# A hybrid attention decoder layer on one core: operand sums made early and kept in DRAM, and four small edits

## The chip, the core and the metric

The kernel runs on one core of one Trainium2 chip. The metric is the device time of one execution in microseconds. Each time is the median of several executions; before the change it is 897.02 us (three executions, 896.83 to 897.15). Engine names are those of the profile: PE is TensorE (matmuls), PEld its weight loads, DVE is VectorE, ACT is ScalarE, POOL is GpSimd, SP is SyncE, which here only issues DMAs.

## What is computed

One decoder layer on 512 tokens of width 1024, in float32. The parts that matter here:

```python
h = layer_norm(x, ln_in_g, ln_in_b)
q_g, k_g, v_g, r_g, a_lr, q_lat, kv_lat, gate_logits = split(h @ w_in)
y_gla = gated_linear_attention(q_g, k_g, v_g, a_lr, r_g) @ w_o_gla       # 4 heads
q = rms_norm(q_lat) @ w_q_b;  kv = rms_norm(kv_lat) @ w_kv_b             # latent attention, 8 heads
s = (q_nope @ k_nope.T + rope(q_rope) @ rope(k_rope).T) * scale          # causal, blocks of 128 queries
y_mla = merge_heads(softmax(s) @ v) @ w_o_mla
g_gla, g_mla = split(sigmoid(gate_logits + b_gate))                      # 1024 channels each
h = layer_norm(alpha * h + (g_gla * y_gla + g_mla * y_mla) @ w_out, ln1_g, ln1_b)
out = layer_norm(alpha * h + square(relu(h @ w_ff1)) @ w_ff2, ln2_g, ln2_b)
```

GLA is the gated linear attention, MLA the latent attention.

## The kernel before, in words

**Precision.** Nearly every product is made of three matmuls. A float32 operand x is split in two parts, hi (rounded, made by ACT) and lo = x - hi (made by DVE); the product is hi*hi + hi*lo + lo*hi, accumulated in PSUM. `split` (L109, its two operations at L111 and L112) does it for activations, `pump` (L177) for weights: L189 is the hi part of a weight block, L190 the lo part.

**The weight stream.** All weight blocks (512 KB each, mostly) stand in one list, `stream`. `fetch` issues their loads on SP's queue (L174) into three buffers (`wraw`), `pump(i)` brings the list to block i and somewhat beyond. `gemm_fm` (matmuls at L245 to L247, 512 tokens moving) and `gemm_tm` (L278 to L280, weights moving) call it before each use, and once more in the middle of the evacuation of their results.

**Order.** The program is written as one main thread of GEMMs and several generators (`spawn`, `tick`, `finish`); each `tick` lets the first two to four generators go one step, so that their small instructions fall between the matmuls. On top of that, a scheduler reorders each engine's instructions by a timeline that it simulates; `tc.issue_after(x)` holds the instructions inside it behind x. On the chip each engine then runs its list strictly in that order.

**Stages**, by their time in the profile: input LayerNorm and latent projections (to 47 us), the q and k products of GLA (47 to 94), v and r (94 to 213), the four GLA heads worked through beside these and the next stage (`gla_levels`: a scan in eight doubling steps, on POOL at L677 and L678, ACT at L682, DVE at L684 and L694, PE at L738), the GLA gates as two GEMMs of 8 blocks (213 to 273), the MLA gates (to 316), rotary queries and the output projection of GLA (from 316 and 320), the MLA heads (354 to 509), output projection and LN1 (to 572), the MLP (to 844), and the last projection (to 887) with LN2.

**Operand sums of the MLA gates.** The MLA gates are computed by a scheme of seven half-size products instead of eight (`unit` L1007, matmuls at L1028 to L1030). It needs sums and differences of quarters of the operand h (`op_sums`, L975): DVE adds the hi and lo part of h (L980), forms four combinations per pair of channel blocks (L984 to L987), and each is split again (L111, L112). `h_sums` runs it beside the two GEMMs of the GLA gates; `u_load("g1", "t1")` ahead of these GEMMs loads two weight blocks on SP and has POOL issue two further loads that are added onto them (L1005).

**Rotary queries.** `mla_qr` (L813) computes the rotary part of four heads' queries; on evacuation DVE does three `rope` operations (L498 to L500) and POOL one for each of the four token blocks. The next GEMM is the first half of the GLA output projection.

**Scores.** `mla_head` (L859) works over four blocks of 128 queries. Block i reads n = 128(i+1) keys; the first block's five matmuls (L871 to L875) are done 256 keys wide. The causal mask is a sixth, bf16 matmul (L876).

**LN1.** `ln_transpose` (L414) transposes the normalised rows on PE (L421); ACT writes the hi part (L424), DVE the float32 copy (L428) and the lo part (L429), eight channel blocks for each half of the tokens.

**The end.** The last 128 tokens of the last projection are done in three column groups of 512, 256 and 256 (L1413 to L1415). Each is added to the residual (L1417), its statistics are taken (L1419), and `ln2` (L1208) applies LN2 in two halves of 512 columns (L1220, L1221) and stores them (L1222).

Of the kernel before, what the change touches and what calls it, by code (L numbers as in the profile page):

```python
# [52 lines left out]
def tile_hybrid_block(ctx: ExitStack, tc: tile.TileContext, I, out, dbg=None):  # L53
# [360 lines left out]
    def ln_transpose(rows, g, b, outs, hf, alt=False, n="h0"):  # L414
        tk = slice(hf * 256, (hf + 1) * 256)
        for k in range(NK):
            if len(outs) <= k:
                outs.append(A([P, 2, T], F32R, n) if n == "h0" else (B([P, T], F32R, n), B([P, T], F32R, n)))
            p = MM() if alt and k in (4, 5) else PX()
            for i in range(2):  # L420
                nc.tensor.transpose(p[:, i * P:(i + 1) * P], rows[2 * hf + i][:, k * P:(k + 1) * P], ident)  # L421
            tmp = B([P, 256], F32, "lnt")
            hi, lo = part(outs[k], 0, tk), part(outs[k], 1, tk)
            ha = act(hi, p[:, :256], AF.Identity, scale=g[:, k:k + 1], bias=b[:, k:k + 1])  # L424
# [388 lines left out]
    def mla_qr(g):  # L813
        qst = []

        def ev_qr(a, j, ps):
            src = ps[:, :4 * ROPE].rearrange("p (h c) -> p h c", c=ROPE)
            csb = cs2[:, a, None, :].to_broadcast([P, 4, ROPE])
            snb = sn2[:, a, None, :].to_broadcast([P, 4, ROPE])
            t1 = B([P, 4, ROPE], F32, "rt1")  # L820
            t2 = B([P, 4, ROPE], F32, "rt2")
            rope(src, csb, snb, t1, t1, t2)
            q2 = B([P, 4, 2, ROPE], F32R, "q2")
            split(t1, q2[:, :, 0, :], q2[:, :, 1, :], scale=scale)
# [12 lines left out]
        return spawn(tr())  # L837
# [21 lines left out]
    def mla_head(h, hl, qn, kn, vt):  # L859
        for _ in range((0 if h == MH - 1 else STAG) * hl):  # L860
            yield
        KK, qs = KKs[0], QS[h]
        Ps = []
        P02 = B([P, T], F32, "P02")
        for i in range(NT):
            n = P * (i + 1)
            nn = max(n, 2 * P)
            c = slice(i * P, (i + 1) * P)
            p = PX()
            o = p[:, :nn]  # L870
            mm(o, qn[:, 0, c], kn[:, 0, :nn], start=True, stop=False)  # L871
            mm(o, qn[:, 0, c], kn[:, 1, :nn], start=False, stop=False)
            mm(o, qn[:, 1, c], kn[:, 0, :nn], start=False, stop=False)
            mm(o, qs[:, c], KK[:, 0, :nn], start=False, stop=False)
            mm(o, qs[:, c], KK[:, 1, :nn], start=False, stop=False)  # L875
# [24 lines left out]
        while vt[NT - 1] is None:  # L900
            yield
        o = PX()
        for j in range(NT):
            c = slice(hl * P, (hl + 1) * P)
            vh, vl = vt[j][:, 0, c], vt[j][:, 1, c]
            if j == 0:
                ph, pl, od = PT0[:, 0, :], PT0[:, 1, :], o
            elif j == 1:
                ph, pl, od = PT1[:, 0, :384], PT1[:, 1, :384], o[:, 128:]
            elif j == 2:  # L910
                ph, pl, od = PT2[:, 0, :], PT2[:, 1, :], o[:, 256:]
            else:
                ph, pl, od = PT1[:, 0, 384:], PT1[:, 1, 384:], o[:, 384:]
            mm(od, vh, ph, start=j == 0, stop=False)
            mm(od, vh, pl, start=False, stop=False)
            mm(od, vl, ph, start=False, stop=j == NT - 1)
        yield
        om = A([P, 2, T], F32R, "omT")
        st["om"] = split(o, om[:, 0, :], om[:, 1, :])
        omT[h] = om  # L920


    def ln_in1():
# [9 lines left out]
        yield  # L933
        yield from ln_transpose(xt, g_in, b_in, hT, 1, alt=False)

    t_ln1 = spawn(ln_in1())
    t_prep = None
    for hf in range(2):
# [133 lines left out]

    hops = []

    def h_sums():
        yield from op_sums(hT,
                           lambda: [[B([P, 2, 256], F32R, "sh") for _ in range(2)] for _ in range(2)], hops)

    t_h = spawn(h_sums())
    u_load("g1", "t1")  # L1080
    for mb in range(2):
        gemm_fm(PL["g", 0, mb], hT, T, lambda a, ps: gate(0, 4 * mb + a, ps, slice(0, T)))
    finish(*t_gla)

    def after(op):
# [119 lines left out]
            yield  # L1205


    def ln2(tt, bst=None):  # L1208
# [130 lines left out]
    for ci in range(FC):  # L1339
# [34 lines left out]
        else:  # L1374
# [29 lines left out]
            gemm_tm(PL["f2last"], hid, T, ev_res, tts=(2,))  # L1404
            spawn(ln2(2))
            tt, r, bst = 3, res[3], S([P, 4, 6], F32, "bst4")
            for c0, n in ((0, T), (T, 256), (T + 256, 256)):
                acc = MM()[:, :n]
                ws = slice(c0 % T, c0 % T + n)
                for k in range(nb):  # L1410
                    hi, lo = weights(PL["f2last"][c0 // T], k)
                    xh, xl = hid[k][:, 0, tt * P:], hid[k][:, 1, tt * P:]
                    mm(acc, xh, hi[:, ws], start=k == 0, stop=False)  # L1413
                    mm(acc, xh, lo[:, ws], start=False, stop=False)
                    mm(acc, xl, hi[:, ws], start=False, stop=k == nb - 1)  # L1415
                    tick(None)
                vtt(r[:, c0:c0 + n], acc, r[:, c0:c0 + n], op=ALU.add)  # L1417
                for j in range(c0 // 256, (c0 + n) // 256):
                    nc.vector.bn_stats(bst[:, j, :], r[:, j * 256:(j + 1) * 256])  # L1419
            finish(spawn(ln2(3, bst)))  # L1420


# [46 lines left out]
```

## Time and profile before

| | |
|---|---|
| median of the executions | 897.02 us |
| the profiled execution | 896.5 us |
| its span, first to last instruction | 894.7 us |
| PE busy | 877.5 us (98%) |
| DVE busy | 614.5 us (69%) |
| ACT busy | 445.1 us (50%) |
| POOL busy | 170.4 us (19%) |
| HBM | 107 GB/s over the span |

The profile is one execution. Its span leaves out 1.8 us around the first and the last instruction. PE's ends of matmuls are modelled, so that back-to-back matmuls overlap in the records; how long one really takes is the distance between the starts of two neighbours. An idle time of PE of half a microsecond or so shows as a wait, a smaller one only in the distance between starts.

### The profile page before, as it was taken

Reading aid. Unit: us, or ns where it says so; the run is one execution under the profiler, and the core shown is the slowest. Engines: PE = TensorE matmul, PEld = TensorE weight load, DVE = VectorE, ACT = ScalarE, POOL = GpSimd, SP = SyncE. Lnnn points to the kernel's source line nnn. Section 1 sums busy time; section 2 is a strip of 40 time slices with the busy share of each in tenths; the row PEclk is TensorE's granted clock in tenths of the full one; section 3 lists DMA queues with packets and bytes.
Section 4 is the critical chain, followed back from the end, with each engine's and each line's share of the span. In section 5 each row is a group of like instructions: output and inputs, shape, how many; then the busy total and the mean of one; then the engine's idle time right before and its main releaser. Section 6 shows DMA issues by size and latency. Waiting matters only on the chain.

```text
span 894.7 us, 12542 instructions
## 1 busy us (share of the span) xinstructions
PE 877.5 (98%) x4796; PEld 760.5 (85%) x4796; DVE 614.5 (69%) x1003; ACT 445.1 (50%) x757; POOL 170.4 (19%) x190
## 2 busy tenths in 40 slices
PE   6999999999999999999999999999999999999996
PEld 5988888888889988888888888988888888889986
DVE  7835855577775745747756797997556646787866
ACT  6455543443546543535645423366457546656810
POOL 1003442444531010100000002103400520141000
PEclk9999999999999999999999999999999999999999
DMA  7314413216325723112207618004950991399312
GB/s 246 122 47 163 131 60 95 71 48 152 84 71 175 197 87 102 49 55 58 95 25 260 210 48 305 3 0 118 314 135 3 271 257 35 76 231 236 117 62 82
DMA packets 73037, 109.41 MB, mean 122 GB/s; under 512 B 7904, under 2 KB 42080, under 8 KB 72976
## 3 DMA queue, kind: packets, MB, share of 16 engines
q1 hardware_dynamic: 57520, 76.62, 27.1%
q0 software_dynamic: 13536, 28.32, 13.8%
q10 hardware_dynamic: 1920, 3.66, 1.2%
q8 instruction: 38, 0.62, 0.3%
q14 instruction: 23, 0.19, 0.1%
HBM read 91.28 MB, written 4.72 MB: 107 GB/s over the span
## 4 chain that ended last, share of the span: by engine, by line
PE 97%; DVE 1%; DMA 1%; ACT 0%; issue 0%; DVEq 0%
PE mm L245 12%; PE mm L247 12%; PE mm L246 12%; PE mm L278 7%; PE mm L279 7%; PE mm L280 7%; PE mm L1030 3%; PE mm L1029 3%; PE mm L1028 3%; PE px L1288 2%; PE px L1287 2%; PE px L1286 2%; PE px L738 2%; PE mm L1288 2%; PE mm L1287 2%; PE mm L1286 2%
## 5 line engine op out<-in xcount | busy, mean ns | idle before, releaser
L190 DVE TENSOR_TENSOR wlo<-wraw,whi 128x1024 fp32r<-128x1024 f32 (+1 forms) x98 | 110.4, 1127 | 110.0 <-ACT whi L189 102.4
L189 ACT ACTIVATE whi<-wraw 128x1024 fp32r<-128x1024 f32 (+1 forms) x98 | 93.9, 959 | 97.9 <-PE mm L246 48.9
L245 PE MATMUL mm<-h,whi 128*128 128x512 f32 x288 | 112.7, 392 | 0.0
L246 PE MATMUL mm<-h,whi 128*128 128x512 f32 x288 | 112.4, 390 | 0.0
L247 PE MATMUL mm<-h,wlo 128*128 128x512 f32 x288 | 107.1, 390 | 0.0
L1305 POOL DMA_DIRECT2D res<-ev x42 | 37.4, 1003 | 177.9 <-ACT ev L1303 143.6
L245 PEld LDWEIGHTS mm<-h,whi 128*128 128x128 f32 x288 | 54.0, 188 | 11.0
L246 PEld LDWEIGHTS mm<-h,whi 128*128 128x128 f32 x288 | 54.1, 188 | 10.8
L247 PEld LDWEIGHTS mm<-h,wlo 128*128 128x128 f32 x288 | 53.9, 188 | 11.0
L279 PE MATMUL mm<-wlo,h 128*128 128x512 f32 x128 | 50.3, 393 | 0.0
L280 PE MATMUL mm<-whi,h 128*128 128x512 f32 x128 | 50.1, 392 | 0.0
L190 DVE TENSOR_TENSOR wlo<-wq,whi 128x1024 fp32r<-128x1024 f32 x30 | 36.7, 1225 | 19.4 <-ACT whi L189 19.4
L278 PE MATMUL mm<-whi,h 128*128 128x512 f32 x128 | 49.7, 403 | 0.0
L677 POOL TENSOR_TENSOR rp<-rp 128x256 f32<-128x256 f32 x32 | 31.6, 988 | 61.1 <-ACT E L682 44.8
L189 ACT ACTIVATE whi<-wq 128x1024 fp32r<-128x1024 f32 x30 | 31.7, 1058 | 19.7 <-PE mm L1029 11.4
L189 ACT ACTIVATE xh<-wraw 128x1024 fp32r<-128x1024 f32 (+1 forms) x28 | 27.4, 984 | 27.8 <-PE mm L280 16.3
L684 DVE TENSOR_TENSOR M<-E,qk 128x512 f32<-128x512 f32 x32 | 27.8, 868 | 14.1 <-ACT E L682 14.1
L406 POOL TENSOR_TENSOR mv<-mv,mhalf 128x1 f32<-128x1 f32 x4 | 4.6, 1155 | 172.3 <-DVE mv L405 172.3
L190 DVE TENSOR_TENSOR xl<-wraw,xh 128x1024 fp32r<-128x1024 f32 (+1 forms) x28 | 31.3, 1130 | 8.5 <-ACT xh L189 8.4
L1028 PE MATMUL mm<-sh,whi 128*128 128x256 f32 x128 | 36.2, 283 | 0.0
L1029 PE MATMUL mm<-sh,whi 128*128 128x256 f32 x128 | 36.2, 283 | 0.0
L1030 PE MATMUL mm<-sh,wlo 128*128 128x256 f32 x128 | 36.2, 283 | 0.0
(419 smaller groups left out, 2576.9 us busy)
## 6 DMA issues: line engine op xcount, KB each, us to landing
wraw<-in_w_in_dram SPq DMA_DIRECT2D x38, 512.0 KB, 3.5
wraw<-in_w_ff_dram SPq DMA_DIRECT2D x36, 512.0 KB, 5.1
wq<-in_w_ff_dram POOLq DMA_DIRECT2D x26, 512.0 KB, 9.7
res<-ev POOLq DMA_DIRECT2D x42, 256.0 KB, 9.2
wraw<-in_w_o_gla_dram SPq DMA_DIRECT2D x8, 512.0 KB, 3.7
wraw<-in_w_o_mla_dram SPq DMA_DIRECT2D x8, 512.0 KB, 3.5
wraw<-in_w_out_dram SPq DMA_DIRECT2D x8, 512.0 KB, 3.8
wq<-in_w_in_dram SPq DMA_DIRECT2D x6, 512.0 KB, 6.1
```

What stands on the lines that cost most here:

```text
L189: st["ins"] = act(hi[:, :nk, :n], raw[:, :nk, :n], AF.Copy)
L190: st["lo"] = vtt(lo[:, :nk, :n], raw[:, :nk, :n], f(hi[:, :nk, :n]), op=ALU.subtract)
L245: mm(o, hi[:, c], xh, start=first, stop=False)
L246: mm(o, hi[:, c], xl, start=False, stop=False)
L247: mm(o, lo[:, c], xh, start=False, stop=last)
L278: mm(o, xh, hi[:, :n], start=opens, stop=False, skip_group_check=share)
L279: mm(o, xh, lo[:, :n], start=False, stop=False, skip_group_check=share)
L280: mm(o, xl, hi[:, :n], start=False, stop=last, skip_group_check=share)
L1028: mm(oa, hi[:, k, c], xh, start=opens and k == 0 and a == 0, stop=False, skip_group_check=True)
L1029: mm(oa, hi[:, k, c], xl, start=False, stop=False, skip_group_check=True)
L1030: mm(oa, lo[:, k, c], xh, start=False, stop=k == 3, skip_group_check=True)
L1305: nc.gpsimd.dma_start(res[tt + t][:, j * T:(j + 1) * T], e, accum_op=ALU.add)
```

## The change

Six edits:

1. The operand sums are made by a new generator `h_early`, started before the k product, with buffers of another pool. Each split part (128x512, 256 KB) is stored to DRAM on SP's queue, 16 stores. `h_load` takes the place of `h_sums`: 16 loads on SP's queue into the buffers that `unit` reads.
2. `u_load("g1", "t1")` moves from ahead of the two GEMMs of the GLA gates to between them.
3. `mla_qr`: ahead of the first `rope`, `pump` splits the next weight blocks, and every `rope` is held behind the last lo part.
4. `mla_head`: the first query block's five matmuls are 128 keys wide.
5. LN1: for odd channel blocks ACT writes the float32 copy as well.
6. The last 256 columns: ACT copies the residual into PSUM ahead of time, the matmuls accumulate on it, and the statistics and the first LN2 operation read PSUM; the addition is gone. The first LN2 operation of these tokens covers 768 and 256 columns.

```diff
@@ ln_transpose
-            if alt and k % 2:
+            if (alt or n == "h1") and k % 2:
                 act(tmp, p[:, :256], AF.Identity, scale=g[:, k:k + 1], bias=b[:, k:k + 1])
@@ ev_qr in mla_qr
+            if a == 0:
+                pump(PL["qr", g]["idx"][-1] + 1)
             t1 = B([P, 4, ROPE], F32, "rt1")
             t2 = B([P, 4, ROPE], F32, "rt2")
-            rope(src, csb, snb, t1, t1, t2)
+            with tc.issue_after(st["lo"].ins):
+                rope(src, csb, snb, t1, t1, t2)
@@ mla_head
-            nn = max(n, 2 * P)
-            o = p[:, :nn]
-            mm(o, qn[:, 0, c], kn[:, 0, :nn], start=True, stop=False)
+            o = p[:, :n]
+            mm(o, qn[:, 0, c], kn[:, 0, :n], start=True, stop=False)
...
@@ main thread, q and k
+    def h_early():
+        for p in range(4):
+            raw = [B([P, T], F32, "hraw") for _ in range(2)]
+            for i in range(2):
+                h = hT[2 * p + i]
+                vtt(raw[i], f(h[:, 0]), f(h[:, 1]), op=ALU.add)
+            yield
+            a11, a12, a21, a22 = raw[0][:, :256], raw[1][:, :256], raw[0][:, 256:], raw[1][:, 256:]
+            X = [B([P, 2, 256], F32, "hx") for _ in range(2)]
+            vtt(X[0][:, 0], a21, a22, op=ALU.subtract)
+            vtt(X[0][:, 1], X[0][:, 0], a11, op=ALU.subtract)
+            vtt(X[1][:, 0], a12, X[0][:, 1], op=ALU.add)
+            vtt(X[1][:, 1], a11, a21, op=ALU.subtract)
+            yield
+            for x in X:
+                xs = [B([P, 2, 256], F32R, "sh") for _ in range(2)]
+                split(x, *xs)
+                hsd.append([DR([P, 2, 256], "hsd") for _ in range(2)])
+                for t, d in zip(xs, hsd[-1]):
+                    nc.sync.dma_start(d, f(t))
+                yield
     gemm_fm(PL["q"], hT, T, ev_q)
     t_lat2 = spawn(latents2())
+    t_he = spawn(h_early())
     gemm_fm(PL["k"], hT, T, ev_k)
@@ main thread, GLA gates
-    t_h = spawn(h_sums())
+    def h_load():
...
+                xh, xl = [B([P, 2, 256], F32R, "sh") for _ in range(2)]
+                for t, d in zip((xh, xl), hsd[2 * p + i]):
+                    nc.sync.dma_start(f(t), d)
...
+    finish(t_he)
+    spawn(h_load())
+    gemm_fm(PL["g", 0, 0], hT, T, lambda a, ps: gate(0, a, ps, slice(0, T)))
     u_load("g1", "t1")
-    for mb in range(2):
-        gemm_fm(PL["g", 0, mb], hT, T, lambda a, ps: gate(0, 4 * mb + a, ps, slice(0, T)))
+    gemm_fm(PL["g", 0, 1], hT, T, lambda a, ps: gate(0, 4 + a, ps, slice(0, T)))
@@ ln2
+        w = T if end is None else D - 256
+        for src, c in ((r[:, :w], slice(0, w)), (r[:, w:] if end is None else end, slice(w, D))):
+            stt(r[:, c], src, mv[:, 0:1], bg[:, c], op0=ALU.subtract, op1=ALU.mult)
         for j in range(2):
             c = slice(j * T, (j + 1) * T)
-            stt(r[:, c], r[:, c], mv[:, 0:1], bg[:, c], op0=ALU.subtract, op1=ALU.mult)
             stt(r[:, c], r[:, c], mv[:, 1:2], bb[:, c], op0=ALU.mult, op1=ALU.add)
@@ last 128 tokens
+            end = PX()[:, :256]
+            with tc.issue_after(st["ins"].ins):
+                act(end, r[:, D - 256:], AF.Copy)
             for c0, n in ((0, T), (T, 256), (T + 256, 256)):
-                acc = MM()[:, :n]
+                last = c0 > T
+                acc = end if last else MM()[:, :n]
...
-                    mm(acc, xh, hi[:, ws], start=k == 0, stop=False)
+                    mm(acc, xh, hi[:, ws], start=k == 0 and not last, stop=False, skip_group_check=last)
...
-                vtt(r[:, c0:c0 + n], acc, r[:, c0:c0 + n], op=ALU.add)
-                for j in range(c0 // 256, (c0 + n) // 256):
-                    nc.vector.bn_stats(bst[:, j, :], r[:, j * 256:(j + 1) * 256])
+                if not last:
+                    vtt(r[:, c0:c0 + n], acc, r[:, c0:c0 + n], op=ALU.add)
+                    acc = r[:, c0:c0 + n]
+                for j in range(n // 256):
+                    nc.vector.bn_stats(bst[:, c0 // 256 + j, :], acc[:, j * 256:(j + 1) * 256])
```

More of the change, by code (lines that the diff above doesn't have):

```diff
@@ L866, in mla_head @@
             n = P * (i + 1)
-            nn = max(n, 2 * P)
             c = slice(i * P, (i + 1) * P)
             p = PX()
-            o = p[:, :nn]
-            mm(o, qn[:, 0, c], kn[:, 0, :nn], start=True, stop=False)
[L872 to L875, printed above, removed]
+            o = p[:, :n]
+            mm(o, qn[:, 0, c], kn[:, 0, :n], start=True, stop=False)
+            mm(o, qn[:, 0, c], kn[:, 1, :n], start=False, stop=False)
+            mm(o, qn[:, 1, c], kn[:, 0, :n], start=False, stop=False)
+            mm(o, qs[:, c], KK[:, 0, :n], start=False, stop=False)
+            mm(o, qs[:, c], KK[:, 1, :n], start=False, stop=False)
             mm(p[:, c], identb, negb, start=False, stop=True)
@@ L1073, in tile_hybrid_block @@
     hops = []
-    def h_sums():
-        yield from op_sums(hT,
-                           lambda: [[B([P, 2, 256], F32R, "sh") for _ in range(2)] for _ in range(2)], hops)
-    t_h = spawn(h_sums())
+    def h_load():
+        for p in range(4):
+            o = {0: (0, 0), 1: (1, 0), 4: (1, 1)}
+            o = {ph: tuple(part(hT[2 * p + i], w, slice(256 * h, 256 * h + 256)) for w in range(2))
+                 for ph, (i, h) in o.items()}
+            for i in range(2):
+                xh, xl = [B([P, 2, 256], F32R, "sh") for _ in range(2)]
+                for t, d in zip((xh, xl), hsd[2 * p + i]):
+                    nc.sync.dma_start(f(t), d)
+                o[(2, 5)[i]], o[(3, 6)[i]] = (xh[:, 0], xl[:, 0]), (xh[:, 1], xl[:, 1])
+            hops.append(o)
+            yield
+    finish(t_he)
+    spawn(h_load())
+    gemm_fm(PL["g", 0, 0], hT, T, lambda a, ps: gate(0, a, ps, slice(0, T)))
     u_load("g1", "t1")
-    for mb in range(2):
-        gemm_fm(PL["g", 0, mb], hT, T, lambda a, ps: gate(0, 4 * mb + a, ps, slice(0, T)))
+    gemm_fm(PL["g", 0, 1], hT, T, lambda a, ps: gate(0, 4 + a, ps, slice(0, T)))
     finish(*t_gla)
@@ L1205, in residual1, with ln2 @@
             yield
-    def ln2(tt, bst=None):
+    def ln2(tt, bst=None, end=None):
         mv = S([P, 2], F32, "mv")
@@ L1412, in tile_hybrid_block @@
                     xh, xl = hid[k][:, 0, tt * P:], hid[k][:, 1, tt * P:]
-                    mm(acc, xh, hi[:, ws], start=k == 0, stop=False)
-                    mm(acc, xh, lo[:, ws], start=False, stop=False)
-                    mm(acc, xl, hi[:, ws], start=False, stop=k == nb - 1)
+                    mm(acc, xh, hi[:, ws], start=k == 0 and not last, stop=False, skip_group_check=last)
+                    mm(acc, xh, lo[:, ws], start=False, stop=False, skip_group_check=last)
+                    mm(acc, xl, hi[:, ws], start=False, stop=k == nb - 1, skip_group_check=last)
                     tick(None)
-                vtt(r[:, c0:c0 + n], acc, r[:, c0:c0 + n], op=ALU.add)
-                for j in range(c0 // 256, (c0 + n) // 256):
-                    nc.vector.bn_stats(bst[:, j, :], r[:, j * 256:(j + 1) * 256])
-            finish(spawn(ln2(3, bst)))
+                if not last:
[3 more added lines that the diff above has]
+                    nc.vector.bn_stats(bst[:, c0 // 256 + j, :], acc[:, j * 256:(j + 1) * 256])
+            finish(spawn(ln2(3, bst, end)))
 _FLAT = {
```

1 line of the change is left out of this document (added).

## The prediction

> **What bounds the kernel now.** I read the page first (busy shares and the chain of work that ended last), then the view of waits, the windows of five stages, and PE's timeline at every place where the distance between two starts exceeds that of such a pair elsewhere. The page:
>
> ```profile
> span 894.7 us, 12542 instructions
> PE 877.5 (98%) x4796; PEld 760.5 (85%) x4796; DVE 614.5 (69%) x1003; ACT 445.1 (50%) x757; POOL 170.4 (19%) x190
> PE 97%; DVE 1%; DMA 1%; ACT 0%; issue 0%; DVEq 0%
> ```
>
> PE is the bound, and 97% of the chain is PE's. Only three things move the end: less work on PE, a gap of PE that closes or opens, or the tail after the last matmul. The windows (columns: length, busy time and instructions of PE, PEld, DVE, ACT, POOL, then clock, DMA share, GB/s):
>
> ```profile
> 0.00:20.00 20.00, 11.34 (x57) 10.54 (x58) 14.72 (x34) 13.12 (x22) 1.78 (x7) 1.00 0.75 248
> 60.00:100.00 40.00, 40.00 (x188) 33.26 (x187) 23.11 (x44) 25.35 (x48) 13.20 (x15) 1.00 0.44 145
> 200.00:250.00 50.00, 49.43 (x279) 42.16 (x278) 40.05 (x70) 24.91 (x46) 23.81 (x25) 1.00 0.42 106
> 880.00:895.00 15.00, 7.64 (x57) 7.12 (x55) 7.66 (x16) 0.00 (x0) 0.92 (x1) 0.87 0.19 72
> ```
>
> The idle time of PE lies in the first 20 us, which no edit touches, and in the last 7, which edit 6 touches. Between them gaps are small. These two are among PE's longest in the view of waits (waiting line, releaser: total, times, longest):
>
> ```profile
> PE px L738 <- DVE SD L694: 0.5, 1, 0.5
> PE mm L247 <- DVE wlo L190: 0.5, 1, 0.5
> ```
>
> So no edit can win much. A measurement of this kernel tells about 0.2% (1.8 us) from no change; the forecast is near that size.
>
> **The change part by part.** I sum against the profiled execution, 896.5 us (span 894.7 and 1.8 around it), then add the 0.5 by which the median, 897.02, stands above it.
>
> *Scores (edit 4).* Eight heads times five matmuls shrink from 256 to 128 columns, on PE, in the middle of the chain. Rows of the same widths:
>
> ```profile
> 362.26 0.28 PE L873 MATMUL px<-qn,qn 128*128 128x256 f32 x1
> 362.38 0.28 PE L874 MATMUL px<-KK,QS 128*128 128x256 f32 x1
> ...
> 390.62 0.22 PE L914 MATMUL px<-PT,mv 128*128 128x128 f32 x1
> 390.68 0.28 PE L915 MATMUL px<-PT,mv 128*128 128x128 f32 x1
> 390.79 0.28 PE L916 MATMUL px<-PT,mv 128*128 128x128 f32 x1
> ```
>
> A 256-column matmul moves the next start by 0.12 us; a 128-column one by 0.06 when the neighbour ahead was wide (L914 to L915) and by 0.11 when it was narrow too (L915 to L916): the next weights are not there sooner. Per head four matmuls gain 0.01 and one 0.06, 0.10 to 0.12 with the rounding of the rows: 8 x 0.11 = **0.9 us**. Ends: 0 if the weight pace takes all, and 40 x 0.06 = 2.4 if all run at the short distance. The trace's row is the nearer one, since all five stand in a row.
>
> By the Trainium skill, page "TensorE: Matmul & The Clock Gate", section "Back-to-back issue gap", pairs of weight load and matmul sustain about 81 ns each at 128 columns. From that figure an estimate of 40 x (120 - 81) ns = 1.6 us would stand in place of the 0.9; the row of 0.11 us speaks against it.
>
> *Rotary queries (edit 3).* Two orders of DVE's and ACT's work before the first block of the GLA output projection:
>
> ```profile
> 319.19 1.06 ACT L189 ACTIVATE whi<-wraw 128x1024 fp32r<-128x1024 f32 x1 [1.85 <-PE mm L280]
> ...
> 320.03 0.42 DVE L498 TENSOR_TENSOR rt<-mm,cs 128x256 f32<-128x256 f32 x1 [2.96 <-PE mm L280]
> ...
> 320.77 1.22 DVE L190 TENSOR_TENSOR wlo<-wraw,whi 128x1024 fp32r<-128x1024 f32 x1
> ...
> 320.90 0.39 PE L245 MATMUL mm<-ogT,whi 128*128 128x512 f32 x1
> 321.13 0.40 PE L246 MATMUL mm<-ogT,whi 128*128 128x512 f32 x1
> 322.04 0.50 PE L247 MATMUL mm<-ogT,wlo 128*128 128x512 f32 x1 [0.51 <-DVE wlo L190]
> ```
>
> Two 512-column matmuls stand 0.23 apart (320.90 to 321.13), so 0.91 holds a stall of 0.68. With the hi part done at 319.19 + 1.06 = 320.25, the lo part ahead of the rope can start at 320.3 in place of 320.77 and free PE 0.47 earlier: **0.5 us**, within 0.3 and the whole 0.68. The rope then comes 1.2 us later; its PSUM bank and POOL's fourth operation follow, and the rotated queries are used first from 354 on, so that is covered. If a later GEMM wanted that bank at once, it would cost those 1.2 us.
>
> *Operand sums (edits 1 and 2).* What leaves the GLA gates, in the view of the tiles there (duration min/median/max in ns):
>
> ```profile
> L980 DVE TENSOR_TENSOR hraw<-h x8: 677/707/1103, 214.5 to 250.2; 128x512 f32<-128x512 f32 x8
> L987 DVE TENSOR_TENSOR hx<-hraw x4: 412/414/418, 218.0 to 253.1; 128x256 f32<-128x256 f32 x4
> L112 DVE TENSOR_TENSOR sh<-hx,sh x6: 677/682/1129, 233.1 to 257.8; 128x512 fp32r<-128x512 f32 x6
> L111 ACT ACTIVATE sh<-hx x6: 612/619/633, 232.5 to 256.1; 128x512 fp32r<-128x512 f32 x6
> ```
>
> 8 x 0.71 + 16 x 0.41 (four lines like L987) + 8 x 0.68 = 17.7 us of DVE and 8 x 0.62 = 5.0 of ACT move from a stage where DVE is busy 40.05 of 50 us to one where it is busy 23.11 of 40 and ACT 25.35. PE's work doesn't change; the gain is the one stall that these operations cause:
>
> ```profile
> 241.33 1.73 DVE L112 TENSOR_TENSOR sh<-hx,sh 128x512 fp32r<-128x512 f32 x2
> 242.98 1.11 DVE L684 TENSOR_TENSOR M<-E,qk 128x512 f32<-128x512 f32 x1
> ...
> 243.85 0.40 PE L247 MATMUL mm<-h,wlo 128*128 128x512 f32 x1
> 244.78 0.43 PE L738 MATMUL px<-M 128*128 128x64 f32 x2 [0.54 <-DVE SD L694]
> ```
>
> 0.93 less 0.23 is a stall of 0.7 that the 1.73 us of `sh` ahead of M and SD cause. I take **0.6**: next late is E on ACT, which feeds M. From above I allow 0.9 (further distances in this stage that exceed the rule by 0.05 to 0.1), from below -1, if the scan loses its place.
>
> *LN1 (edit 5).* Two stalls, one after each group of transposes:
>
> ```profile
> 565.90 1.03 PE L421 MATMUL px<-ca,res 128*128 128x128 f32 x8
> 567.26 0.74 PE L245 MATMUL mm<-h,xh 128*128 128x256 f32 x4 [0.33 <-ACT h L424]
> 567.84 0.90 PE L421 MATMUL px<-ca,res 128*128 128x128 f32 x4
> 568.63 0.38 PE L246 MATMUL mm<-h,xh 128*128 128x256 f32 x1
> ```
>
> The first waits for ACT's first hi parts and stays. Where DVE sets the second, ACT's copies relieve it; but ACT itself gets more work. I take **0.2**, between -0.3 (the order on ACT is worse by one copy) and 0.5.
>
> *The end (edit 6).*
>
> ```profile
> 887.67 0.42 DVE L1417 TENSOR_TENSOR res<-mm,res 128x256 f32<-128x256 f32 x1 [1.99 <-PE mm L1415]
> 888.13 0.43 DVE L1419 BATCH_NORM_STATS2 bst<-res 128x6 f32<-128x256 f32 x1
> ```
>
> The addition and the step behind it, 0.46 us, fall out of the tail. LN2's first operation covers the same 1024 columns as 768 and 256, so the second half's store can't start earlier, and the first one starts later behind the wider operation without being last. **0.4**, between 0.3 and 0.46. ACT's copy has until 887 and ACT is idle in the last 15 us (0.00 above).
>
> *New waits.* SP gets 16 stores and 16 loads of 256 KB, and DVE's early sums meet the weight splits and POOL:
>
> ```profile
> latd<-latT SPq DMA_DIRECT2D x5, 512.0 KB, 3.9
> ...
> 68.69 1.23 DVE L190 TENSOR_TENSOR wlo<-wraw,whi 128x1024 fp32r<-128x1024 f32 x1 [6.57 <-ACT whi L189]
> 71.09 2.33 DVE L190 TENSOR_TENSOR wlo<-wraw,whi 128x1024 fp32r<-128x1024 f32 x1 [1.18 <-ACT whi L189]
> ```
>
> A store that waits for its sum holds the weight loads queued behind it on SP. The nearest row is 3.9 us to landing for twice the size, and the DMA engines are busy 0.44 of that stage, so the blocks queued behind it keep a margin. DVE waits 6.57 and 1.18 us for its next hi part there; a sum of 0.7 fits, but while POOL ran (the second row) the same operation took 2.33 in place of 1.23, which shows that a margin of a microsecond can vanish once. I take **-0.3**, from 0 down to -3 (two or three such collisions).
>
> Sum: 0.9 + 0.5 + 0.6 + 0.2 + 0.4 - 0.3 = **2.3 us**. 896.5 - 2.3 = 894.2 profiled, and with 0.5 a median of **894.7 us**. Its own range, adding the terms' ends only in part, is 893.4 to 895.7.
>
> **The rivals.**
>
> *All scores at the short distance.* If weights run ahead for all five matmuls, edit 4 gives 2.4 in place of 0.9: 894.7 - 1.5 = 893.2. For it: the 0.06 of L914. Against it: L915, the only narrow one behind a narrow one. This is also the direction of the page's figure above.
>
> *Stalls return elsewhere.* Every edit changes the list order of several engines, and a wait of this size can come from any one operation that stands a place later. If new stalls of 0.5 to 0.7, like the two that go, appear in two or three places, the 1.3 us of edits 1, 2, 3 and 5 (0.6 + 0.5 + 0.2) are lost and 0.2 more: 894.7 + 1.5 = 896.2. For it: all stalls that I count have this size. Against it: DVE becomes emptier where it was fullest. That is also how it would be if the sums didn't relieve the stage.
>
> *The scan waits for a DMA (slower).*
>
> ```profile
> 245.32 1.12 POOL L677 TENSOR_TENSOR rp<-rp 128x256 f32<-128x256 f32 x1 [0.74 <-ACT E L682]
> 246.53 0.95 POOL L678 TENSOR_TENSOR rp<-rp 128x256 f32<-128x256 f32 x1
> ...
> 217.41 20.85 SPq L174 DMA_DIRECT2D wraw<-in_w_in_dram  x4
> ```
>
> In the changed order the two accumulating DMAs of `u_load("g1", "t1")` stand on POOL between these two operations of the last head's scan, and must wait for their two loads on SP. Those now stand behind up to 16 loads of the sums and the weight blocks, instead of ahead of them. SP issues the weight loads of this stage spread over 20.85 us, held by their buffers, so what stands behind them is held too. At 230 I put some 14 of the 16 loads of 256 KB ahead of them, 3.7 MB; at the 106 GB/s and 0.42 share of the window, a full share is 106 / 0.42 = 252 GB/s, so 3.7 MB take 15 us: landing near 245 to 248. POOL waits there; L678, then E, M, SD and L738 follow, and PE runs its list in order, so beyond the slack each microsecond costs one. The slack is that to 246.5; from a landing past 251 the 4.5 us exceed the gains by 0.2% of the time. At that point: 894.7 + 4.5 = 899.2 us.
>
> **How the numbers follow.** Forecast 0.53, scores short 0.07, stalls return 0.25, the scan waits 0.15. Faster (under 895.2): 0.07 and 0.48 of the forecast's 0.53, together 0.55. Within 0.2% (895.2 to 898.8): 0.05 and 0.25, together 0.30. Slower: 0.15. The range runs from 893.0, just under the short scores, to 897.6, which is 1.4 beyond the returned stalls; outside it lies the waiting scan and little else.
>
> **What would show it.** Right: distances of 0.11 between four of five score matmuls of the first block, no stall at the first L247 of the GLA output projection, none at the L738 near 244, about 0.46 less between the last matmul and the end. Wrong: distances of 0.06 or 0.12 there; a POOL wait for a DMA inside the last scan with PE waiting at L738; waits of L247 or L245 for `wlo` or `wraw` between 60 and 115 us. If PE's idle time falls by less than a microsecond and stalls of that size stand in new places, the second rival held.

## The result, and the profile after

The changed kernel takes **893.98 us** (median of 8 executions, 893.63 to 894.66), beside 896.83 us for the kernel before on the same chip (8 executions, 896.16 to 897.47): 2.85 us less, a ratio of 0.9971 with a 95% interval of 0.9962 to 0.998. The forecast was 894.7, from 893.0 to 897.6, with faster as the likeliest.

The page of the changed kernel, the same three lines as before. PE is still the bound, with 1.1 us less busy time; the span is 2.4 us shorter.

```profile
span 892.3 us, 12629 instructions
...
PE 876.4 (98%) x4796; PEld 760.7 (85%) x4796; DVE 610.2 (68%) x994; ACT 449.1 (50%) x766; POOL 166.6 (19%) x190
...
PE 98%; DMA 1%; ACT 0%; DVE 0%; POOLq 0%; DVEq 0%; issue 0%
```

The windows of the changed kernel (columns as before: length, PE, PEld, DVE, ACT, POOL, clock, DMA share, GB/s):

```profile
60.00:100.00 40.00, 40.00 (x188) 33.20 (x187) 32.41 (x62) 27.11 (x52) 12.84 (x13) 1.00 0.58 197
200.00:250.00 50.00, 50.00 (x283) 43.22 (x282) 30.60 (x52) 23.15 (x42) 20.10 (x22) 1.00 0.51 170
```

DVE went from 40.05 to 30.60 us in the GLA gates (the window from 200 to 250 us) and from 23.11 to 32.41 in the 60 to 100 us window, as edit 1 means it to. The view of PE's waits (waiting line, releaser: total, times, longest) has lost two of its rows, L738 for SD and L247 for wlo, and has no new one; these are all:

```profile
PE px L421 <- ACT x L410: 8.3, 1, 8.3
PE mm L278 <- ACT h L424: 0.4, 1, 0.4
PE mm L245 <- ACT h L424: 0.3, 1, 0.3
```

**A ledger.** Both kernels issue 4796 matmuls. So the start of the n-th matmul, counted from the first one, can be compared: where the difference grows, PE lost time, and where it falls, PE gained. In the stretches that the table leaves out it changes by no more than 0.05 us in the changed kernel; exceptions in other kernels are named where they come up. Times are those of the profile before; all differences are in us against the kernel before. The last column has the kernels with one edit alone (edits 1 and 2 together), described below. The ledger compares one profiled execution of each kernel.

| stretch | forecast | changed kernel | the edit alone |
|---|---|---|---|
| 102 to 141, v product | +0.3 (new waits) | **+0.60** | +0.26 (edits 1 and 2) |
| 216 to 277, GLA gates | -0.6 | **-1.13** | -1.13 (edits 1 and 2) |
| 277 to 318, MLA gates | 0 | **-0.20** | -0.20 (edits 1 and 2) |
| 318 to 349, rotary queries | -0.5 | **-0.68** | -0.67 (edit 3) |
| 349 to 490, scores | -0.9 | **-0.53** | -0.65 (edit 4) |
| 542 to 589, LN1 | -0.2 | **-0.10** | -0.09 (edit 5) |
| last matmul's start to the end | -0.4 | **-0.39** | -0.36 (edit 6) |

The changed kernel's column adds up to -2.4, the span's difference. The medians differ by 2.85 because the profiled execution before, 896.5 us, was 0.3 faster than its median.

### The profile page after: what moved, and what is told of

It is laid out like the page before. It is cut to its first block, busy times and chain, and to the rows that moved or that the text cites. A ratio compares the mean times of both kernels' runs of the same rounds, so it can differ in the third digit from the quotient of the medians.

```text
span 892.3 us, 12629 instructions
## 1 busy us (share of the span) xinstructions
PE 876.4 (98%) x4796; PEld 760.7 (85%) x4796; DVE 610.2 (68%) x994; ACT 449.1 (50%) x766; POOL 166.6 (19%) x190
## 4 chain that ended last, share of the span: by engine, by line
PE 98%; DMA 1%; ACT 0%; DVE 0%; POOLq 0%; DVEq 0%; issue 0%
PE mm L245 13%; PE mm L247 13%; PE mm L246 13%; PE mm L278 7%; PE mm L279 7%; PE mm L280 7%; PE mm L1057 3%; PE mm L1055 3%; PE mm L1056 3%; PE px L1326 2%; PE px L1327 2%; PE px L1325 2%; PE px L738 2%; PE mm L1326 2%; PE mm L1325 2%; PE mm L1327 2%
## 5 line engine op out<-in xcount | busy, mean ns | idle before, releaser
L245 PE MATMUL mm<-h,whi 128*128 128x512 f32 x288 | 113.0, 392 | 0.0
L246 PE MATMUL mm<-h,whi 128*128 128x512 f32 x288 | 112.5, 391 | 0.0
L247 PE MATMUL mm<-h,wlo 128*128 128x512 f32 x288 | 107.4, 391 | 0.0
L247 PEld LDWEIGHTS mm<-h,wlo 128*128 128x128 f32 x288 | 54.1, 188 | 11.1
L246 PEld LDWEIGHTS mm<-h,whi 128*128 128x128 f32 x288 | 54.2, 188 | 10.8
L245 PEld LDWEIGHTS mm<-h,whi 128*128 128x128 f32 x288 | 54.1, 188 | 10.8
L278 PE MATMUL mm<-whi,h 128*128 128x512 f32 x128 | 49.5, 402 | 0.1
L684 DVE TENSOR_TENSOR M<-E,qk 128x512 f32<-128x512 f32 x32 | 25.8, 807 | 14.3 <-ACT E L682 14.3
```

The source lines that it names most:

```text
L245: mm(o, hi[:, c], xh, start=first, stop=False)
L246: mm(o, hi[:, c], xl, start=False, stop=False)
L247: mm(o, lo[:, c], xh, start=False, stop=last)
L278: mm(o, xh, hi[:, :n], start=opens, stop=False, skip_group_check=share)
```

## The experiments

Each kernel was run in turn with the kernel before on the same chip, with 11 executions of each changed program (5 of `e10_late`) beside 27 or 33 of the kernel before. Except for the operand sums, a single edit is worth less than the interval of a comparison (about 0.9 us either way), so the medians show at most the direction and the ledger shows the place. The first 50 us vary between executions by up to 0.95 us and carry no verdict.

**Theory:** the gains are the named gaps of PE, each edit closes its own, and they add; the loss at v is the early sums' splits ahead of the evacuation of v on DVE. **Rival:** the gaps are a matter of how the instruction lists fall, and single edits would show other gaps, or none.

### One edit at a time

Scores 128 columns wide, nothing else changed:

```diff
-            nn = max(n, 2 * P)
-            o = p[:, :nn]
+            o = p[:, :n]
```

> Before with edit 4 alone. Weight pace: a narrow score matmul still takes 0.11 us where its neighbour is narrow, so each head gains about 0.08 us and the whole 0.5 to 0.7 us (median near 896.2). Short distance: 0.06 us each, 2.4 us (near 894.4). If the gain in the changed kernel was only that its list came out in another order: within 0.2 us of the kernel before.

Measured 896.03 us beside 896.80, ratio 0.9993 (0.9984 to 1.0002); in the ledger -0.65 between 349 and 490 us, and nothing else beyond the first 50 us. The weight pace held. One head of the changed kernel, PE's timeline (start, duration, line):

```profile
428.35 0.40 PE L246 MATMUL mm<-latT,whi 128*128 128x512 f32 x1
428.58 0.23 PE L873 MATMUL px<-qn,qn 128*128 128x128 f32 x1
428.64 0.27 PE L874 MATMUL px<-qn,qn 128*128 128x128 f32 x1
428.76 0.28 PE L875 MATMUL px<-qn,qn 128*128 128x128 f32 x1
428.87 0.28 PE L876 MATMUL px<-KK,QS 128*128 128x128 f32 x1
428.98 0.27 PE L877 MATMUL px<-KK,QS 128*128 128x128 f32 x1
429.10 0.23 PE L878 MATMUL px<-negb,identb 128*128 128x128 bf16 x1
```

The first moves the next start by 0.06 us, the others by 0.11 to 0.12 (0.112 on average), beside 0.12 each at 256 columns: 0.06 and 4 x 0.006 make 0.08 a head, which agrees with 0.65 for eight. In the changed kernel the same heads gain 0.12 less in all, most of it between 370 and 397 us; the cause of that is not shown.

The weight split ahead of the rope:

```diff
+            if a == 0:
+                pump(PL["qr", g]["idx"][-1] + 1)
-            rope(src, csb, snb, t1, t1, t2)
+            with tc.issue_after(st["lo"].ins):
+                rope(src, csb, snb, t1, t1, t2)
```

> Before with edit 3 alone. If the weight split ahead of the rope is the cause, the 0.5 us wait of L247 for wlo goes and with it 0.5 to 0.7 us (near 896.2). Rival, the rope behind the split makes something else late: 0 or a loss, with a new PE gap between 322 and 355 us.

Measured 896.15 beside 896.80, ratio 0.9991 (0.9982 to 1.0001); ledger -0.67 between 318 and 349 us and no new gap. The changed kernel's rows, ACT, DVE and PE in the same place as before:

```profile
318.42 1.06 ACT L189 ACTIVATE whi<-wraw 128x1024 fp32r<-128x1024 f32 x1 [1.85 <-PE mm L280]
...
319.51 1.23 DVE L190 TENSOR_TENSOR wlo<-wraw,whi 128x1024 fp32r<-128x1024 f32 x1 [3.22 <-ACT whi L189]
320.95 1.23 DVE L190 TENSOR_TENSOR wlo<-wraw,whi 128x1024 fp32r<-128x1024 f32 x1 [0.22 <-ACT whi L189]
322.09 0.42 DVE L498 TENSOR_TENSOR rt<-mm,cs 128x256 f32<-128x256 f32 x1
...
320.35 0.40 PE L246 MATMUL mm<-ogT,whi 128*128 128x512 f32 x1
320.79 0.73 PE L247 MATMUL mm<-ogT,wlo 128*128 128x512 f32 x2
```

The lo part starts right behind the hi part, and L247 comes 0.44 behind L246 instead of 0.91: 0.47 gained, the term forecast. Two lo parts now stand ahead of the rope, so it comes 2.8 us later, counted from ACT's first row (322.09 - 318.42 = 3.67 beside 320.03 - 319.19 = 0.84). Most of the other 0.2 comes from what the later rope moves. Before, the sixteen transposes of the queries stood between the wide matmuls in seven small groups (328.54 to 333.59); in the changed kernel they stand in two groups of eight. The wide matmul behind such a group moves the next start by 0.28 to 0.31 instead of 0.23 us. With that surplus counted to the group, the sixteen cost PE 1.55 us before and 1.40 in the changed kernel, 0.15 less. The first group of eight:

```profile
328.19 0.79 PE L835 MATMUL px<-identr,q 128*128 128x128 f32 x8
328.81 0.46 PE L245 MATMUL mm<-ogT,whi 128*128 128x512 f32 x1
329.12 0.39 PE L246 MATMUL mm<-ogT,whi 128*128 128x512 f32 x1
```

Which half of edit 3 does it? The kernel before with the split put first in the program, but the rope not held:

```diff
+            if a == 0:
+                pump(PL["qr", g]["idx"][-1] + 1)
```

> Before with half of edit 3: the weights are split ahead of the rope by the program, but the rope is not held behind the last lo part. If the hold makes the gain: no gain, 896.8, and the 0.5 us wait of L247 for wlo stays. If the place of the split in the program is enough: as edit 3 alone, 0.65 less, 896.15.

Measured 896.71 beside 896.73, ratio 0.9999 (0.9991 to 1.0008). Ledger +0.04 between 318 and 349 us. DVE's timeline of this kernel has the old order:

```profile
320.26 0.42 DVE L498 TENSOR_TENSOR rt<-mm,cs 128x256 f32<-128x256 f32 x1 [2.96 <-PE mm L280]
...
321.00 1.21 DVE L190 TENSOR_TENSOR wlo<-wraw,whi 128x1024 fp32r<-128x1024 f32 x1
```

The scheduler put the rope back ahead; the hold is what changes the list.

LN1's float32 copies of odd blocks on ACT:

```diff
-            if alt and k % 2:
+            if (alt or n == "h1") and k % 2:
```

> Before with edit 5 alone. Forecast's term: 0.2 us less, with the second stall after the transposes near 568 us shorter. Rival, nothing at all: DVE did not set that stall; then the distances after both groups of transposes stay as they were.

Measured 896.67 beside 896.80, ratio 0.9998 (0.9989 to 1.0007); ledger -0.09 between 542 and 589 us. The first stall stays (1.36 from the transposes to L245 in both kernels), and so does 0.33 of waiting for ACT. The second stays too: the second transpose after 567.84 still moves the next start by 0.29 us. What is gained is that two of the four transposes there, which took 0.165 each, now stand with the next group, where each takes 0.11. So half of the forecast's 0.2 came, near its place, but not by a shorter stall; that DVE set that stall is not shown.

The end of the last product:

```diff
+            with tc.issue_after(st["ins"].ins):
+                act(end, r[:, D - 256:], AF.Copy)
...
+                acc = end if last else MM()[:, :n]
...
+                if not last:
+                    vtt(r[:, c0:c0 + n], acc, r[:, c0:c0 + n], op=ALU.add)
```

> Before with edit 6 alone. Forecast's term: 0.3 to 0.46 us less from the last matmul's start to the end. Rival, the wider first LN2 operation gives part of it back: 0.1 to 0.3 less.

Measured 896.62 beside 896.80, ratio 0.9999 (0.999 to 1.0008). From the last matmul's start to the end it is 0.36 us shorter. (Its profiled execution was the slowest of its eleven, 898.7, with 0.95 us more in the first 50 us and 1.33 between 542 and 589 us, which the edit doesn't touch; the others took 896.26 to 896.97.) DVE's timeline in the changed kernel:

```profile
885.60 0.43 DVE L1464 BATCH_NORM_STATS2 bst<-px 128x6 f32<-128x256 f32 x1 [0.31 <-PE px L1458]
886.07 0.26 DVE L1252 BATCH_NORM_AGGREGATE mv<-bst 128x2 f32<-128x24 f32 x1
...
886.43 1.01 DVE L1257 SCALAR_TENSOR_TENSOR res<-res,mv,bc 128x768 f32<-128x768 f32 x1
887.36 0.48 DVE L1257 SCALAR_TENSOR_TENSOR res<-px,mv,bc 128x256 f32<-128x256 f32 x1
887.88 1.42 DVE L1260 SCALAR_TENSOR_TENSOR res<-res,mv,bc 128x512 f32<-128x512 f32 x2
```

The statistics follow the last matmul directly, which is worth the 0.46 us of the addition; from the aggregate to the second LN2 operation it takes 1.81 instead of 1.68 us (888.60 to 890.28 before), so 0.13 goes back. That leaves 0.33. The ledger's 0.36 and 0.39 are a little more because the profiled execution before has a long tail: `e1_scores`, `e2_rotary` and `e3_ln1`, which leave the tail alone, are 0.05 to 0.06 us shorter there.

### The operand sums

Edit 1 alone, with the two weight blocks `t1` left ahead of both GEMMs, and then edits 1 and 2 together:

```diff
     finish(t_he)
     spawn(h_load())
+    u_load("g1", "t1")
     gemm_fm(PL["g", 0, 0], hT, T, lambda a, ps: gate(0, a, ps, slice(0, T)))
-    u_load("g1", "t1")
```

> Before with edit 1 alone: early sums, their loads, but the two weight blocks t1 stay ahead of both GEMMs of the GLA gates. If the relief of DVE there is worth the 1.1 us seen between 214 and 268 us, and the late evacuation of v at 124 us costs 0.5, the net is 0.5 to 0.8 less. Rival, edit 2 is needed for the gain because the loads stand behind t1: no gain or a loss, with PE waits between 214 and 273 us.

> Before with edits 1 and 2. If the operand sums alone make the gain and t1's place is indifferent: 0.5 to 0.8 us less, as without edit 2. If the gain comes from t1's place: over 0.3 us better than without edit 2.

Measured 896.00 (ratio 0.9990, 0.9981 to 0.9999) and 895.44 (ratio 0.9987, 0.9978 to 0.9996), both beside 896.83. In the GLA gates the ledgers read -1.03 and -1.13, in the MLA gates -0.20 in both, at v +0.27 and +0.26. So the sums make the gain, and edit 2 a tenth of a microsecond. The stall of 0.7 ahead of L738 is gone (PE's timeline of the changed kernel, the same two matmuls as at 243.85 and 244.78 before, now 0.23 apart):

```profile
244.39 0.40 PE L247 MATMUL mm<-h,wlo 128*128 128x512 f32 x1
244.62 1.00 PE L738 MATMUL px<-M 128*128 128x64 f32 x8
```

By their medians the two kernels lie 0.56 apart, as the second branch of the expectation has it; the rest of that is not in the stage of edit 2, and 0.20 of it stands at 809 us in the profile without edit 2. The mirror image, the changed kernel with edit 2 undone:

> The changed kernel with edit 2 undone: the two weight blocks t1 ahead of both GEMMs of the GLA gates. If their place matters by itself, as the medians of edit 1 alone and edits 1 and 2 (896.00 and 895.44) would have it: 0.5 us more, 894.5. If it doesn't, as PE's distances in their profiles say: within 0.2 us of the changed kernel.

Measured 894.62 beside 896.73, ratio 0.9978 (0.9969 to 0.9987): 2.11 less than before, where the changed kernel had 2.85. The median is where the first branch puts it, but its place is another: against the changed kernel the profile loses 0.10 in the GLA gates, and 1.02 after 800 us, with a wait that no other profile shows (view of PE's waits); edit 1 alone lost 0.20 there:

```profile
PE px L1057 <- DVE wlo L190: 0.5, 1, 0.5
```

The lists of instructions are the same there as in the changed kernel. Its eleven times fall into two groups, 894.2 to 894.6 and 895.0 to 895.7; the profiled execution (895.56) is of the second. Whether that loss makes the second group, and what `t1` early has to do with it, stays open.

In the changed kernel `t1` did what the slower rival feared in order, but not in time (views of SP's and POOL's timelines):

```profile
230.65 3.79 SPq L1110 DMA_DIRECT2D sh<-hsd  x8
238.42 0.38 SPq L174 DMA_DIRECT2D wraw<-in_w_in_dram  x1
238.85 1.01 SPq L1030 DMA_DIRECT2D wq<-in_w_in_dram  x2
...
249.00 1.17 POOL L677 TENSOR_TENSOR rp<-rp 128x256 f32<-128x256 f32 x1 [2.51 <-ACT E L682]
250.11 1.47 POOL L1032 DMA_DIRECT2D wq<-in_w_in_dram  x1
251.09 1.15 POOL L678 TENSOR_TENSOR rp<-rp 128x256 f32<-128x256 f32 x1
251.66 1.86 POOL L1032 DMA_DIRECT2D wq<-in_w_in_dram  x1
```

The loads of the sums were all issued by 234.4, `t1` at 238.85, and POOL came to it 11 us later. POOL waited for no DMA. Issuing the first put 0.9 us between two scan operations that stood 0.1 apart before; the second fell into the time in which the scan waits for ACT anyway. L678 came at 251.09 instead of 246.53, and PE did not wait.

### The loss at v

From the first of four L746 to the wide matmul behind them it is 1.21 us in the changed kernel and 0.68 before. PE's and DVE's rows before, and then those of the changed kernel:

```profile
123.43 1.03 PE L746 MATMUL px<-M 128*128 128x256 f32 x4
124.11 0.58 PE L278 MATMUL mm<-whi,h 128*128 128x512 f32 x1
...
120.80 0.41 DVE L112 TENSOR_TENSOR vl<-mm,vh 128x256 fp32r<-128x256 f32 x1
```

```profile
123.54 1.10 PE L746 MATMUL px<-M 128*128 128x256 f32 x4
124.75 0.47 PE L278 MATMUL mm<-whi,h 128*128 128x512 f32 x1
...
120.76 1.10 DVE L112 TENSOR_TENSOR sh<-hx,sh 128x512 fp32r<-128x512 f32 x1
...
122.72 0.68 DVE L684 TENSOR_TENSOR M<-E,qk 128x512 f32<-128x512 f32 x1
123.32 1.95 DVE L112 TENSOR_TENSOR vl<-mm,vh 128x256 fp32r<-128x256 f32 x5
```

L278 writes a PSUM buffer that the evacuation of v (`vl`) has to free. Before, `vl` began at 120.80; now a split of the early sums stands in that place and `vl` begins at 123.32. In the changed kernel and in the four others with the same sums (`e5_sums`, `e6_sums_t1`, `e8_interleave`, `e11_t1_first`) L278 starts 1.43 to 1.44 us behind the first `vl`, whatever the time of that: it follows `vl`.

Of the changed kernel's 0.60, 0.42 lies here (the 0.53, less 0.11 that the next matmul gets back), and 0.17 in one distance ahead of an L738 at 107.73 us. The four others lose about 0.29 here, nothing there, and 0.25 to 0.27 in all. Their lists are the same up to here, so how late DVE runs differs between executions; what made it later in this one is not shown.

Three kernels move the sums: earlier (started ahead of the q product), closer together, and later.

```diff
+    t_he = spawn(h_early())
     gemm_fm(PL["q"], hT, T, ev_q)
     t_lat2 = spawn(latents2())
-    t_he = spawn(h_early())
```

> The changed kernel with the early sums started ahead of the q product instead of the k product, so that their last splits stand ahead of the evacuation of v on DVE by a wide margin. Theory, the last splits at 116.8 and 120.8 us hold the evacuation of v and PE at 124.75 us: the 0.5 us come back, near 893.5. Rival, that gap comes from the scan's order and not from the splits: same as the changed kernel, 894.0, or new gaps between 50 and 95 us and a loss of up to 1 us.

Measured 896.16 beside 896.83, ratio 0.9991 (0.9982 to 1.0000). The theory's gap went and the rival's new ones came: against the changed kernel the ledger gives 0.60 back at v, and loses 2.37 between 50 and 102 us, over twice what the expectation allowed, where the sums meet POOL's long operations. ACT's, DVE's, POOL's and PE's rows of this kernel:

```profile
70.18 0.63 ACT L111 ACTIVATE sh<-hx 128x512 fp32r<-128x512 f32 x1 [0.83 <-DVE hx L950]
70.72 1.07 ACT L521 ACTIVATE qk<-mm 128x512 f32<-128x512 f32 x2
...
68.64 1.51 DVE L950 TENSOR_TENSOR hx<-hx,hraw 128x256 f32<-128x256 f32 x1
...
66.91 6.58 POOL L591 TENSOR_TENSOR g<-g,az 128x512 f32<-128x512 f32 x4 [41.21 <-ACT az L588]
...
71.35 0.50 PE L245 MATMUL mm<-h,whi 128*128 128x512 f32 x1 [1.12 <-ACT qk L521]
```

The combination that takes 0.41 us elsewhere took 1.51 while POOL ran; ACT's split waited for it, the evacuation of q waited behind the split, and PE waited 1.12 us for the evacuation. This stop costs 1.4 of the 2.37. The next one, 0.6, is L247 waiting for the lo part of a weight block, whose split took 2.28 us beside the same work of POOL (from 70.07) where 1.2 is usual.

```diff
                 for t, d in zip(xs, hsd[-1]):
                     nc.sync.dma_start(d, f(t))
-                yield
+            yield
```

> The changed kernel with the two splits of each pair of the early sums in one step, so that the last pair's splits stand on DVE well before the evacuation of v. Theory, these splits hold that evacuation: the 0.6 us lost between 94 and 127 us shrink to under 0.2, median near 893.5. Rival, the gap at 124.75 us is the scan's own or the stream of weights': still 0.5 to 0.6 there, 894.0.

Measured 895.41 beside 896.73, ratio 0.9985 (0.9976 to 0.9994): worse than the changed kernel, with 1.22 more lost at v. The theory's gain did not come, and the loss is another than the rival's: `vl` does start without a split ahead, at 122.69, but PE now waits for M (PE's and POOL's timelines of this kernel):

```profile
125.14 1.10 PE L746 MATMUL px<-M 128*128 128x256 f32 x4 [1.52 <-DVE M L684]
...
98.20 3.74 POOL L678 TENSOR_TENSOR rp<-rp 128x256 f32<-128x256 f32 x1 [0.90 <-DMA hsd<-sh]
```

The same scan step took 0.61 us in the changed kernel, at 97.11. Behind this long step the scan's next E came 1.4 us later than in the changed kernel (101.98 beside 100.55), and its last M 1.6 us later (124.30 beside 122.72).

```diff
         for p in range(4):
+            for _ in range(6 if p == 3 else 0):
+                yield
             raw = [B([P, T], F32, "hraw") for _ in range(2)]
```

> The changed kernel with six empty steps ahead of the last pair of the early sums, so that its splits come behind the first evacuation of v on DVE. Theory, the splits ahead of the evacuation cost PE the 0.5 us: they come back here too, near 893.5, if nothing later waits for the moved ones. Rival, the gap moves along to the second evacuation or stays: 894.0.

Measured 893.92 beside 896.73, ratio 0.9965 (0.9953 to 0.9978). The four L746 and the next wide matmul take 0.68 again:

```profile
123.14 1.03 PE L746 MATMUL px<-M 128*128 128x256 f32 x4
123.82 0.58 PE L278 MATMUL mm<-whi,h 128*128 128x512 f32 x1
```

The ledger at v reads -0.05 against the kernel before, 0.65 better than the changed kernel and 0.3 better than the four others with its sums, and no later stretch differs by more than 0.01. L278 now starts 1.69 us behind the first `vl`, without a wait. So the loss at the evacuation came from the place of the last pair's work on DVE. The median is 2.81 below the kernel before, as the changed kernel's 2.85: the gain shows in the distances of PE and not in five executions.

### Can the narrow matmuls be hidden?

The 0.06 us behind a wide matmul suggested taking wide and narrow matmuls in turn, the first block's with the last block's:

```diff
+            for m in range(5):
+                for i in blocks:
...
+                        with tc.issue_after(x.ins):
+                            x = mm(done[i][:, :n], *ops[m], start=m == 0, stop=False)
...
-        for i in range(NT):
+        for i in (3, 0, 1, 2):
+            if i not in done:
+                scores(*((3, 0) if i == 3 else (i,)))
```

> The changed kernel with the first and the last block of the scores done together, a 512-column matmul and a 128-column one in turn (the blocks then go 3 and 0, 1, 2). If weights are loaded ahead under the wide matmul, each narrow one takes 0.06 instead of 0.11 us: 8 x 4 x 0.05 = 1.6 us less, near 892.4. If a load can only begin when the matmul ahead has started, the next wide one waits instead: about the same as the changed kernel, 894.0.

Measured 897.50 beside 896.83, ratio 1.0006 (0.9998 to 1.0015). PE's timeline of this kernel, groups of four in turn wide and narrow, then the mask matmuls:

```profile
354.22 0.84 PE L886 MATMUL px<-KK,QS 128*128 128x512 f32 x4
354.91 0.28 PE L888 MATMUL px<-negb,identb 128*128 128x128 bf16 x2
```

Two pairs take 0.69 us, 0.345 a pair; in separate runs a wide one takes 0.23 and a narrow one 0.11, together 0.34. The narrow ones do take 0.06, but the wide one behind them takes 0.285, so the sum is the same. The 3.2 us that this kernel loses between 349 and 490 us are waits for DVE in later heads (1.5 us of L886 and 1.3 of L914 for PT); whether the new order of the blocks or the two PSUM buffers held at once make them was not tried apart.

## Why the prediction was right

The direction and the time (894.7 beside 893.98) held, and so did the mechanism of every edit but the fifth. The rival of returning stalls holds for one stretch only, v. That the sum came so near is in part luck, as its terms show:

- **Scores, 0.9 forecast, 0.65 alone (0.53 in the changed kernel).** The weight pace was read rightly, though the distance, 0.112, lies between the 0.11 that was named as right and the 0.12 named as wrong. The term was mis-sized: four of five matmuls gain 0.006 and not the 0.01 with its rounding, so a head gains 0.08 and not 0.11. The rival of short distances failed. L915 was not the only narrow one behind a narrow one: the kernel before also has transposes of 128 columns that follow each other at 0.065 to 0.087 (L832), which the choice left out. Where the Trainium skill, page "TensorE: Matmul & The Clock Gate", section "Back-to-back issue gap", has about 81 ns for a pair of weight load and 128-column matmul, these float32 pairs took 110 to 115; the transposes of L832 come near its figure.
- **Rotary queries, 0.5 forecast, 0.68 measured.** The wait for wlo shrank by the forecast 0.47. The 0.2 beside it, 0.15 of it from transposes that now stand together, was not in the working. The rope came 2.8 us later and not 1.2, as two lo parts went ahead; nothing waited for it.
- **Operand sums, 0.6 forecast, 1.33 measured** (1.13 and 0.20). This is the term most wrong. I counted the one stall that the view of waits showed, 0.7 at 243.85. Gaps below half a microsecond went as well: 0.20 behind the four transposes that begin at 245.73, some 0.2 in smaller ones of this stage, and 0.2 in the MLA gates, behind the second group of four transposes (281.17), which held PE 0.19 longer than the first. In the changed kernel these eight stand in four pairs without such a hold; what held them is not shown. My upper end of 0.9 was too low.
- **LN1, 0.2 forecast, 0.10.** Within its bounds, but by another way: the stall that ACT's copies were to relieve stayed, and two transposes moved out of it.
- **The end, 0.4 forecast, 0.36 to 0.39 (0.33 without the long tail of the execution before).** Within its bounds. The 0.13 for the wider LN2 operation was named but not priced.
- **New waits, 0.3 lost forecast, 0.60 in the profile of the changed kernel and about 0.26 in four other kernels with the same sums** (`e5_sums`, `e6_sums_t1`, `e8_interleave`, `e11_t1_first`). The cause was not a store on SP or a weight split, and it lay at 124 us, behind the 60 to 115 us that were named. It was the evacuation of v behind a sum's split, which `e7_sums_at_q` and `e10_late` show; 0.17 of the 0.60 lies elsewhere, as said above.
- **The scan that waits for a DMA** did not happen. Its order was right; the price had `t1` landing near 245 to 248 behind a full queue, while the sums' loads were all issued by 234.4. The slack was misjudged too: the scan's L678 came 4.6 us later than before and PE did not wait, where the price had each microsecond past 246.5 cost one.

That the terms add is shown by the ledger, stretch by stretch: the single edits give -2.8 in all, the changed kernel -2.4, and the differences are the 0.34 more at v and the 0.12 less in the scores. The medians agree (0.77 + 0.65 + 0.13 + 0.18 + 1.39 = 3.1 us beside 2.85), but five intervals of 0.9 us would not show it alone. By the ledger the forecast's 2.3 came near the 2.4 partly because errors cancel, which is luck: the sums gained 0.7 more and the rotary queries 0.2 more, the scores 0.4 less, LN1 0.1 less, and the new waits cost 0.3 more.

## What to carry to other kernels

Where one engine is busy 98%, number its instructions and compare their starts in two traces: the differences sit in a few places and add up to the span's, while medians of single edits drown in scatter. When work is moved off a crowded stage, count every gap there that is wider than such a pair elsewhere, not only the rows of the view of waits; and look in the stage that receives it for the instruction that frees a buffer and now stands behind the moved work. A scheduler may undo an order that is only written in the program; the held kernel and the one without the hold differ by all of the gain.

## What the runs showed of the hardware

A 128-column matmul of split parts (the scores) moves the next start by 0.11 to 0.115 us behind its like and by 0.06 behind a wide one, and the 512-column one behind it then moves the next start by 0.28 to 0.31 instead of 0.23. Taking wide and narrow in turn hides nothing.

Transposes of 128 columns have two paces in the kernel before, though the rows write both as f32. Those of rounded values (L832, against the rounded identity `identr`) take 0.06 behind a wide matmul and 0.065 to 0.087 behind each other; those of float32 values (L801) take 0.11 in either place. Putting them together saves little: with the surplus of the wide matmul behind them, the sixteen of L832 cost 1.55 us in seven groups and 1.40 in two, and those of L801 among 256-column matmuls cost 0.44 for four together and 0.22 for two.

A combination on DVE that usually takes 0.41 us took 1.51 beside POOL's long operations (`e7_sums_at_q`; four of POOL's in 6.58 us, 1.6 each), and POOL's scan step of 0.61 us took 3.74 when the early sums stood closer (`e9_dense`), while DVE worked from 98.42 to 101.47 without a pause. By the Trainium skill, page "SBUF — State Buffer", section "🔬 SBUF: two separate sides", a DVE operation with two SBUF inputs and a GpSimd operation that reads SBUF lock a shared pair of ports against each other for the whole instruction. The long steps agree with that; no run here changed one of the two engines alone.
